# Seven more heads per layer: probabilities times values as one float32 product in place of two split products

## The chip, the cores and the metric

The kernel runs on one core of a Trainium2 chip. The metric is the device time of one execution in microseconds, the median of several runs. Times of single instructions come from one profiled execution of the same kernel.

## The reference, cut to what matters

The program is two transformer blocks on a sequence of 512 tokens, width 1024. The first block has two layers, and each layer is a feed-forward part, a mixer with four groups of attention heads (a: neighbourhood windows, b: low-rank latent, c: difference of two softmaxes, d: grouped queries; four heads of width 64 in each), an output projection, and a second feed-forward part. The second block has one layer with other mixers. What the change touches is the last line of each attention of the first block:

```python
p = jax.nn.softmax(logits, axis=-1).astype(v.dtype)
return jnp.einsum('bhqk,bkhd->bqhd', p, v)
```

All arithmetic is float32. For group a the probabilities of a query are zero outside a window, so there fewer keys count; for group c the weight is the difference of two softmaxes.

## The kernel before

TensorE multiplies the type `float32r` (the code's F32R) at a higher rate than float32, with fewer bits. Most products are therefore split: a number is a high part `hi` (a float32r copy, made on ScalarE) and a low part `lo` (the number minus `hi`, made on VectorE or GpSimd), and the product is three float32r matmuls (`Builder.mm3`, lines 99 to 101; line 442 in the projections; line 323 in the feed-forward parts).

The mixer of a first-block layer is `mix_layer`. The string `PLAN` (line 975) gives the order in which projections and heads are written, and `schedule` interleaves the stages of the heads, up to five at a time. The heads come in the order c0, c1, c2, c3, b0, b1, d0, b2, b3, d1, d2, a0, d3, a1, a2, a3. The framework's scheduler then sets each engine's order from its own estimates, so an edit in one head can move other instructions; each engine runs its own list in order. Between heads the list of TensorE holds projections (line 442), whose weights ScalarE copies (line 88) and GpSimd subtracts (line 89, `wlo`).

A head has three stages. The first builds the transposed queries and keys (line 518 transposes the tiles `dup`; `st` tiles at lines 525 to 539 and 855 to 862). The second computes four blocks of scores (line 549) and their softmax (lines 559 to 563: a maximum `nm` on VectorE, an exponential `p` on ScalarE). The third is `attend` (line 630): for each of the four key blocks it transposes the probabilities into a PSUM bank of the ring `t` of three (line 642), copies them to SBUF as `pth` on ScalarE, and multiplies them by the values. There are two ways to do that. Which one a head takes is told by the list `NATIVE` (line 408):

```python
native = key in NATIVE
vv = None if native else self.split_v(v, c0, h % 2)
# split: split_p, lines 509 and 510, then pv, lines 575 to 579
nc.scalar.activation(out=h[:, a:z], in_=ps[:, a:z], func=AF.Copy)
nc.vector.tensor_tensor(out=l[:, a:z], in0=ps[:, a:z], in1=h[:, a:z].bitcast(F32), op=ALU.subtract)
for e in range(2):
    nc.tensor.matmul(out=ps[:, a:z], lhsT=vv[:, j], rhs=pts[j][e][:, a:z], ...)
nc.scalar.activation(out=y[r], in_=ps[o], func=AF.Copy)
nc.vector.tensor_tensor(out=y[r], in0=ps[r], in1=y[r], op=ALU.add)
# native: line 649, then pv_native, lines 589 and 590
nc.scalar.activation(out=t[:, a:z], in_=ps[:, a:z], func=AF.Copy)
nc.tensor.matmul(out=ps[r, a:z], lhsT=v[:, j, c0:c0 + 64], rhs=pts[j][:, a:z], ...)
nc.scalar.activation(out=y[r], in_=ps[r], func=AF.Copy)
```

The split way puts the high and low parts of a head's 64 value columns side by side in one tile `vv` of 128 columns (line 501 on ScalarE, line 502 on GpSimd), splits the probabilities into `pth` and `ptl`, runs two float32r matmuls for each key block (line 575), and adds the two halves of the result on VectorE (line 579). The native way uses the float32 values and probabilities as they are, with one float32 matmul for each key block (line 589). The profile records such a float32 matmul as two matmuls, each with a weight load.

Before the change nine of the sixteen heads are native: a0, a1, a3, b1, b3, c1, c3, d1, d3. The other seven are split, in both layers. The forgetting attention of the second block is split too (it calls `attend` without a key).

Of the kernel before, what the change touches and what calls it, by code (L numbers as in the profile page):

```python
# [404 lines left out]
NCOPY = ()  # L405
PVA = ()
QKA = ('a3',)
NATIVE = 'a0,a1,a3,b1,b3,c1,c3,d1,d3'.split(',')

NA_WIN = [(0, 2), (0, 3), (1, 4), (2, 4)]  # L410
NA_OFF = [0, 256, 256, 640]
# [2 lines left out]
class Mixer1:  # L414
# [215 lines left out]
    def attend(self, ys, h, probs, v, c0, win=None, key=None):  # L630

        b, nc = self.b, self.nc
        win = win or [(0, 4)] * 4
        native = key in NATIVE
        vv = None if native else self.split_v(v, c0, h % 2)
# [1387 lines left out]
```

## Time and profile before

| | before |
|---|---|
| median of 3 runs | 2501.27 us (2501.06 to 2502.19) |
| profiled execution: time, span of its instructions | 2497.98 us, 2496.2 us |
| granted TensorE clock, mean | 0.992 |
| PE busy, PEld busy | 2387.0 us (96%), 2074.3 us (83%) |
| DVE, ACT, POOL busy | 1817.4 us (73%), 1270.8 us (51%), 710.3 us (28%) |
| mixer of layer 0, of layer 1 | about 395 to 700 us, about 1432 to 1738 us of the span |

PE is TensorE's matmuls, PEld its weight loads, DVE is VectorE, ACT ScalarE, POOL GpSimd. The end of a matmul is modelled in the profile and matmuls overlap, so what a matmul takes of TensorE's time is read from the start of one to the start of the next. In a row of the timeline, "x6" means that six equal records in a row are merged. In brackets at the end stands the idle time of that engine before the instruction, and what ended it.

### The profile page before, as it was taken

Reading aid. Unit: us, or ns where it says so; the run is one execution under the profiler, and the core shown is the slowest. Engines: PE = TensorE matmul, PEld = TensorE weight load, DVE = VectorE, ACT = ScalarE, POOL = GpSimd, SP = SyncE. Lnnn points to the kernel's source line nnn. Section 1 sums busy time; section 2 is a strip of 40 time slices with the busy share of each in tenths; the row PEclk is TensorE's granted clock in tenths of the full one; section 3 lists DMA queues with packets and bytes.
Section 4 is the critical chain, followed back from the end, with each engine's and each line's share of the span. In section 5 each row is a group of like instructions: output and inputs, shape, how many; then the busy total and the mean of one; then the engine's idle time right before and its main releaser. Section 6 shows DMA issues by size and latency. Waiting matters only on the chain. (4 is left out here: it accounts for less than half of the span.)

```text
span 2496.2 us, 39030 instructions
## 1 busy us (share of the span) xinstructions
PE 2387.0 (96%) x14712; PEld 2074.3 (83%) x14712; DVE 1817.4 (73%) x3247; ACT 1270.8 (51%) x2414; POOL 710.3 (28%) x559
## 2 busy tenths in 40 slices
PE   8999999899999999999999999999999999889998
PEld 6899988776778999888999888767889997678778
DVE  7877776976487777787777689745877777855654
ACT  5444456677443444544444566764444445434474
POOL 2221115652212121302111447323011104453232
PEclk9999999999999999999999999999999999999999
DMA  5333333210323333323332432012333324131111
GB/s 166 107 102 102 95 117 102 89 51 16 98 82 107 105 102 89 94 92 107 105 103 68 134 100 90 20 54 85 102 98 105 103 61 155 59 81 43 41 42 64
DMA packets 113884, 220.55 MB, mean 88 GB/s; under 512 B 22192, under 2 KB 33520, under 8 KB 113696
## 3 DMA queue, kind: packets, MB, share of 16 engines
q1 hardware_dynamic: 110288, 217.74, 28.7%
q8 instruction: 115, 1.88, 0.3%
q10 hardware_dynamic: 3408, 0.33, 0.1%
q14 instruction: 73, 0.60, 0.1%
HBM read 209.14 MB, written 8.78 MB: 87 GB/s over the span
## 5 line engine op out<-in xcount | busy, mean ns | idle before, releaser
L88 ACT ACTIVATE whi<-raw 128x1024 fp32r<-128x1024 f32 (+4 forms) x351 | 271.6, 775 | 488.6 <-PE t L323 205.3
L298 POOL TENSOR_TENSOR xl<-xh,xh 128x512 f32<-128x512 f32 x120 | 175.9, 1469 | 718.0 <-DVE wlo L306 368.3
L323 PE MATMUL t<-fh,wlo 128*128 128x256 f32 x1024 | 288.0, 281 | 2.4 <-DVE wlo L306 2.4
L323 PE MATMUL t<-fh,whi 128*128 128x256 f32 x1024 | 287.6, 281 | 0.0
L323 PE MATMUL t<-fl,whi 128*128 128x256 f32 x1024 | 287.6, 281 | 0.0
L99 PE MATMUL acc<-gh,whi 128*128 128x512 f32 x704 | 274.7, 391 | 7.7 <-DVE x L380 5.2
L100 PE MATMUL acc<-gl,whi 128*128 128x512 f32 x704 | 274.5, 390 | 0.0
L101 PE MATMUL acc<-gh,wlo 128*128 128x512 f32 x704 | 274.3, 390 | 0.2 <-DVE wlo L89 0.2
L89 DVE TENSOR_TENSOR wlo<-raw,whi 128x512 fp32r<-128x512 f32 (+3 forms) x277 | 229.8, 830 | 52.7 <-ACT whi L88 51.2
L89 POOL TENSOR_TENSOR wlo<-raw,whi 128x1024 fp32r<-128x1024 f32 (+2 forms) x74 | 167.8, 2270 | 203.5 <-ACT whi L88 190.6
L323 PE MATMUL s<-fh,whi 128*128 128x256 f32 x768 | 216.3, 282 | 8.0 <-DVE wu L326 8.0
L323 PE MATMUL s<-fh,wlo 128*128 128x256 f32 x768 | 215.8, 281 | 0.0
L323 PE MATMUL s<-fl,whi 128*128 128x256 f32 x768 | 215.7, 281 | 0.0
L323 PEld LDWEIGHTS t<-fh,wlo 128*128 128x128 f32 x1024 | 196.4, 192 | 3.1 <-DVE wlo L306 3.0
L305 ACT ACTIVATE whi<-xh 128x512 fp32r<-128x512 f32 x180 | 113.9, 633 | 165.5 <-issue 85.7
L323 PEld LDWEIGHTS t<-fl,whi 128*128 128x128 f32 x1024 | 192.3, 188 | 5.0
L323 PEld LDWEIGHTS t<-fh,whi 128*128 128x128 f32 x1024 | 192.2, 188 | 5.0
L380 DVE SCALAR_TENSOR_TENSOR x<-acc,x 128x512 f32<-128x512 f32 x184 | 126.5, 687 | 64.4 <-PE acc L101 64.0
L306 DVE TENSOR_TENSOR wlo<-xh,whi 128x512 fp32r<-128x512 f32 x180 | 147.5, 819 | 27.9 <-ACT whi L305 27.8
L442 PE MATMUL acc<-whi,xh 128*128 128x256 f32 (+1 forms) x576 | 165.0, 290 | 2.2 <-DVE gate L1140 1.8
L442 PE MATMUL acc<-wlo,xh 128*128 128x256 f32 (+1 forms) x576 | 166.4, 290 | 0.1
L442 PE MATMUL acc<-whi,xl 128*128 128x256 f32 (+1 forms) x576 | 165.9, 290 | 0.0
(724 smaller groups left out, 6535.8 us busy)
## 6 DMA issues: line engine op xcount, KB each, us to landing
xh<-in_ffn_gu_dram SPq DMA_DIRECT2D x240, 256.0 KB
raw<-in_ffn_d_dram SPq DMA_DIRECT2D x128, 256.0 KB
raw<-in_ffn_gu_dram SPq DMA_DIRECT2D x48, 512.0 KB
raw<-in_w2f_dram SPq DMA_DIRECT2D x25, 512.0 KB
raw<-in_ffn_d_dram SPq DMA_DIRECT2D x64, 192.0 KB
xs<-x SPq DMA_DIRECT2D x24, 256.0 KB
raw<-in_a_dram SPq DMA_DIRECT2D x12, 512.0 KB
x<-xs SPq DMA_DIRECT2D x24, 256.0 KB
```

The source lines that it names most:

```text
L88: nc.scalar.activation(out=hi, in_=raw, func=AF.Copy)
L89: (lo_eng or self.lo_eng).tensor_tensor(out=lo, in0=raw, in1=hi.bitcast(F32), op=ALU.subtract)
L99: mm(out=out, lhsT=lh, rhs=rh, start=start, stop=False)
L100: mm(out=out, lhsT=lh, rhs=rl, start=False, stop=False)
L101: mm(out=out, lhsT=ll, rhs=rh, start=False, stop=stop)
L298: eng.tensor_tensor(out=o, in0=x, in1=y, op=op)
L305: nc.scalar.activation(out=hi[:, c], in_=src, func=AF.Copy)
L306: nc.vector.tensor_tensor(out=lo[:, c], in0=src, in1=hi[:, c].bitcast(F32), op=ALU.subtract)
L323: nc.tensor.matmul(out=out, lhsT=x[:, k], rhs=y[:, j], start=start and k == 0 and n == 0, stop=stop and k == 3 and n == 2, skip_group_chec ...
L380: nc.vector.scalar_tensor_tensor(out=x, in0=ps, scalar=0.5, in1=x, op0=ALU.mult, op1=ALU.add)
L442: mm = lambda l, r, st=False, sp=False: nc.tensor.matmul(out=ps[i], lhsT=l, rhs=r, start=st, stop=sp, skip_group_check=True)
```

## The change

The list names all sixteen heads. So the heads a2, b0, b2, c0, c2, d0 and d2 of both layers go the native way.

```diff
-NATIVE = 'a0,a1,a3,b1,b3,c1,c3,d1,d3'.split(',')
+NATIVE = [m + h for m in 'abcd' for h in '0123']
```

What this does to the lists of the engines is shown at three places of layer 0.

VectorE, head c0, while the softmaxes of head c1 and the projections of group b stand beside it. Before:

```order
L753 TENSOR_TENSOR t_948_4755<-t_948_4755,rt_4789 128x8x32
L510 TENSOR_TENSOR ptl_5035<-t_5029,pth_5034 128x512
L466 TENSOR_SCALAR hms_4820<-hms_4820 128x4
L890 TENSOR_SCALAR c_1015_4983<-c_1015_4983,sums_4270,c_nl_4261 128x1
L510 TENSOR_TENSOR ptl_5044<-t_5038,pth_5043 128x512
L465 TENSOR_REDUCE hms_4851<-sq_971_4849 128x4
L892 SCALAR_TENSOR_TENSOR p_4979<-p_4986,c_1015_4983,p_4979 128x512
```

and now:

```order
L753 TENSOR_TENSOR t_948_4755<-t_948_4755,rt_4789 128x8x32
L466 TENSOR_SCALAR hms_4820<-hms_4820 128x4
L890 TENSOR_SCALAR c_1015_4983<-c_1015_4983,sums_4270,c_nl_4261 128x1
L465 TENSOR_REDUCE hms_4851<-sq_971_4849 128x4
L892 SCALAR_TENSOR_TENSOR p_4979<-p_4986,c_1015_4983,p_4979 128x512
```

The subtractions that make `ptl` are gone from between the other work; over the program VectorE's list loses 70 instructions (56 of line 510, 14 of line 579), GpSimd's the 14 of line 502, and ScalarE's the 14 of line 501.

TensorE, the products of head c0 among the projections. Before:

```order
L442 MATMUL acc_5373<-wlo_5431,xh_758_3949 128x256
L575 MATMUL t_5065<-pth_5034,vv_5026 128x512
L575 MATMUL t_5065<-ptl_5035,vv_5026 128x512
L575 MATMUL t_5065<-pth_5043,vv_5026 128x512
L575 MATMUL t_5065<-ptl_5044,vv_5026 128x512
L442 MATMUL acc_5373<-whi_5430,xl_759_3950 128x256
```

and now:

```order
L442 MATMUL acc_5340<-wlo_5399,xh_751_3924 128x256
L589 MATMUL t_5054<-pth_5031,cv_4321 64x512
L589 MATMUL t_5054<-pth_5038,cv_4321 64x512
L442 MATMUL acc_5340<-whi_5398,xl_752_3925 128x256
L442 MATMUL acc_5340<-whi_5398,xh_758_3949 128x256
```

Four float32r matmuls have become two float32 ones of half as many output rows, and they stand some matmuls earlier among the projections.

TensorE, head d0, where the `dup` tiles belong to a later head. Before:

```order
L575 MATMUL t_6439<-pth_6426,vv_6400 128x512
L575 MATMUL t_6439<-ptl_6427,vv_6400 128x512
L518 MATMUL t_6458<-ident_150,dup_6450 128x128
L518 MATMUL t_6458<-ident_150,dup_6452 128x128
L518 MATMUL t_6458<-ident_150,dup_6454 128x128
L518 MATMUL t_6458<-ident_150,dup_6456 128x128
L575 MATMUL t_6439<-pth_6435,vv_6400 128x512
```

and now:

```order
L549 MATMUL s_6418<-st_6316,st_6308 128x512
L589 MATMUL t_6380<-pth_6371,dv_5333 64x512
L518 MATMUL t_6394<-ident_150,dup_6386 128x128
L518 MATMUL t_6394<-ident_150,dup_6388 128x128
L518 MATMUL t_6394<-ident_150,dup_6390 128x128
L518 MATMUL t_6394<-ident_150,dup_6392 128x128
L589 MATMUL t_6380<-pth_6378,dv_5333 64x512
```

The products no longer stand in one run: scores of another head lie between the second and the third, so the four float32 products form three groups.

## Rows read from the trace of the kernel before

**Rows 1.** Stretches: length, busy us of PE, PEld, DVE, ACT, POOL; clock, DMA.
```profile
440.00:530.00 90.00, 81.73 (x570) 72.75 (x570) 88.23 (x222) 61.56 (x142) 62.07 (x54) 0.96 0.27 83
530.00:690.00 160.00, 153.26 (x819) 112.20 (x817) 93.82 (x210) 96.92 (x209) 43.69 (x40) 1.00 0.18 55
1477.00:1567.00 90.00, 79.90 (x565) 71.26 (x564) 89.06 (x214) 59.74 (x138) 61.51 (x52) 0.98 0.24 80
...
450.00:460.00 10.00, 6.94 (x33) 6.21 (x34) 9.88 (x22) 5.92 (x13) 4.39 (x3) 0.66 0.33 107
```

**Rows 2.** Waits of PE, 440 to 690: total us, times, longest.
```profile
PE s L549 <- DVE nm L562: 3.9, 2, 2.5
PE t L642 <- DVE st L526: 2.8, 4, 0.9
PE t L518 <- DVE dup L490: 2.3, 1, 2.3
PE t L642 <- DVE ptl L510: 2.0, 2, 1.7
...
PE t L518 <- DVE y L579: 0.3, 1, 0.3
```

**Rows 3.** The same view of layer 1, 1477 to 1727.
```profile
PE t L642 <- DVE ptl L510: 2.9, 3, 2.0
```

**Rows 4.** Timeline of the split product: start, us, engine, instruction (d0, then a2).
```profile
569.50 0.40 PE L575 MATMUL t<-ptl,vv 128*128 128x512 f32 x1
569.73 0.39 PE L575 MATMUL t<-pth,vv 128*128 128x512 f32 x1
...
649.18 0.34 PE L575 MATMUL t<-ptl,vv 128*128 128x384 f32 x1
649.36 0.29 PE L575 MATMUL t<-pth,vv 128*128 128x256 f32 x1
649.48 0.28 PE L575 MATMUL t<-ptl,vv 128*128 128x256 f32 x1
```

**Rows 5.** Timeline of the native product, with the row behind it (d1, then a1).
```profile
594.51 1.93 PE L589 MATMUL t<-pth,dv 128*64 128x512 f32 x4
596.37 0.50 PE L549 MATMUL s<-st,st 128*128 128x256 f32 x2
596.80 1.07 PE L589 MATMUL t<-pth,dv 128*64 128x512 f32 x2
597.81 1.16 PE L136 MATMUL t<-sel,ysq 128*128 128x128 f32 x8
...
640.37 0.86 PE L589 MATMUL t<-pth,av 128*64 128x384 f32 x2
641.16 0.50 PE L100 MATMUL acc<-xl,whi 128*128 128x512 f32 x1
...
645.07 0.65 PE L589 MATMUL t<-pth,av 128*64 128x256 f32 x2
645.65 1.16 PE L136 MATMUL t<-sel,ysq 128*128 128x128 f32 x8
```

**Rows 6.** Groups by line of VectorE, 440 to 690: busy us, mean ns, idle before.
```profile
L510 DVE TENSOR_TENSOR ptl<-t,pth 128x512 fp32r<-128x512 f32 x24 | 16.3, 684 | 1.3 <-ACT pth L509 1.1
L579 DVE TENSOR_TENSOR y<-t,y 64x512 f32<-64x512 f32 x7 | 4.7, 678 | 0.9 <-ACT y L578 0.9
```

**Rows 7.** The line that makes `vv` on GpSimd: duration min/median/max.
```profile
L502 POOL TENSOR_TENSOR vv<-cv,vv x4: 741/744/752, 405.9 to 1443.7; 128x256 fp32r<-128x256 f32 x4
```

**Rows 8.** Timelines of DVE, POOL and PE where PE stops in layer 0.
```profile
447.24 2.60 DVE L752 TENSOR_TENSOR t<-t,b_cos 128x256 f32<-128x256 f32 x1
...
446.73 2.83 POOL L89 TENSOR_TENSOR wlo<-raw,whi 128x1024 fp32r<-128x1024 f32 x1
...
451.35 0.50 PE L549 MATMUL s<-st,st 96*128 96x512 f32 x1 [2.45 <-DVE nm L562]
...
455.31 1.12 PE L642 MATMUL t<-ident,p 128*128 128x128 f32 x4 [1.71 <-DVE ptl L510]
```

## The prediction

> **What bounds the kernel now.** I read the stretches of the two mixers first, since the change touches nothing else. A mixer has two phases. In the first, 440 to 530 us in layer 0 and 1477 to 1567 in layer 1, VectorE is busy 88.2 and 89.1 of 90 us and TensorE 81.7 and 79.9 [rows 1]: both are full, and TensorE has 8.3 and 10.1 us of idle. In the second, 530 to 690, TensorE is busy 153.3 of 160 us and VectorE 93.8 [rows 1]: TensorE sets the pace, with 6.7 us of idle. So per layer TensorE has some 15.0 us of idle (8.3 + 6.7), and the rest is its own work. Second, the waits of TensorE say who ends that idle time. In layer 0 the softmax maxima take 3.9 us, a query stack of line 526 2.8, a `dup` tile 2.3, `ptl` 2.0 and the addition of line 579 0.3 [rows 2]; in layer 1 `ptl` takes 2.9 [rows 3]. Only `ptl` and line 579 are removed by the change. Third, the timeline tells what the long stops are made of. A VectorE multiply took 2.60 us from 447.24 while a GpSimd subtraction of 2.83 us ran from 446.73, and TensorE then stood 2.45 us for a maximum from VectorE, and soon after 1.71 us for `ptl` [rows 8]. In the ten microseconds of these two stops the granted clock fell to 0.66 [rows 1], a mixture of 1.2 and 2.4 GHz, and was back at 1.00 for the phase behind it.
>
> **The price on TensorE.** Matmul time is counted from start to start.
>
> - Split, 512 columns: 569.50 to 569.73 is 0.23 us [rows 4]; a head has 4 key blocks of 2 matmuls, 8 x 0.23 = 1.84 us.
> - Native, 512 columns: a run of two products (four records) takes 594.51 to 596.37, 1.86 us, and one product by itself 596.80 to 597.81, 1.01 us [rows 5]. Head d1 consists of such a run and two single ones: 1.86 + 1.01 + 1.01 = 3.88 us. In runs alone a head would take 3.72, in single products 4.04. The list of d0 after the change shows one run and two single products, so I take 3.88. A head costs 3.88 - 1.84 = 2.04 us more (1.88 to 2.20).
> - Head a2 has two blocks of 384 columns and two of 256. Split: 649.18 to 649.36 and 649.36 to 649.48, 0.18 and 0.12 us [rows 4], 4 x 0.18 + 4 x 0.12 = 1.20. Native: 640.37 to 641.16 and 645.07 to 645.65, 0.79 and 0.58 us a product [rows 5], 2 x 0.79 + 2 x 0.58 = 2.74. More by 1.54.
> - Per layer six heads of the first kind and one a2: 6 x 2.04 + 1.54 = 13.8 us; both layers **27.6 us** (25.7 to 29.5 with the bounds).
>
> This work lies on TensorE's own list in stretches that it fills to 91% and 96%, so it counts in full, and what follows says how much is given back.
>
> **What is given back.**
>
> - Waits that ended with an instruction that goes: `ptl` 2.0 and 2.9, line 579 0.3, together 5.2 us. Next late in these places is ScalarE's copy `pth`, which came just before `ptl`; it had to be there anyway. I credit **5**; half of it, if the copy holds the bank nearly as long.
> - The clock. It fell after two stops in layer 0, and the second ended with `ptl` [rows 8]. Without it the fall may not come. A share of 0.66 over ten microseconds in which TensorE was busy 6.9 [rows 1] costs 0.34 x 6.9 = 2.3 us; I credit **2** (0 to 2.3).
> - VectorE. In a layer it loses 24 subtractions and seven additions, 16.3 + 4.7 = 21.0 us of the 88.2 + 93.8 that it is busy [rows 6, 1], some 12%, and the four smaller subtractions of a2. Other VectorE results that TensorE waits for come sooner by part of that. Those waits are 3.9 + 2.8 + 2.3 = 9.0 us in layer 0 [rows 2], and I take layer 1 for the same, 18 in all. The bounds are 0 and 18. The two largest follow a VectorE instruction held beside a GpSimd subtraction of weights [rows 8], and those subtractions all stay; the waits for line 526 lie in a phase where VectorE has room. So I take a third, **6**.
> - GpSimd loses 14 subtractions of 0.74 us [rows 7] and ScalarE 14 copies. Both run long before they are needed (a head's `vv` is made while its scores are), nothing on TensorE is seen to wait for them, and I give them nothing. No DMA is added or removed; a few weight loads stand elsewhere in the queue, with no wait of TensorE on them in these stretches.
>
> Sum: 27.6 - 5 - 2 - 6 = **+14.6 us**. The profiled execution took 2498.0 us, so it would take 2512.6; the median stands 3.3 us above it, at 2501.3, and so the forecast is 2515.9, in round numbers **2515 us**.
>
> On the held instruction there is a rule to weigh. The row alone says that one of VectorE's multiplies took 2.60 us while GpSimd was at work [rows 8], and I priced the removal of GpSimd's `vv` at nothing. The Trainium skill, page "SBUF — State Buffer", section "Who interferes with whom", says that VectorE with two inputs in SBUF and a GpSimd instruction that reads SBUF shut each other out for the length of an instruction. The trace agrees in this row: the long multiply ends just after the GpSimd instruction. By that rule the 14 `vv` subtractions could each hold VectorE for up to their own length, 14 x 0.74 = 10.4 us, and the sum would be +9 if TensorE waited for a half of that. It also says that an instruction with at most one SBUF input is not held, and the `ptl` subtraction has one (its other is PSUM), so by it the removed subtractions never were among the held ones. No row shows a `vv` subtraction holding anything that TensorE waited for, so the sum goes without it.
>
> **The rivals.**
>
> *VectorE sets the pace, and the kernel gets faster.* Place: both first phases. For it: 88.2 of 90 us busy there, and the longest stops of TensorE end with VectorE [rows 1, 2]. Then less VectorE work shortens the phase, TensorE's added work fills idle time, and in the second phase the waits go as well. Its most is all the idle time of the mixer, 15.0 us a layer, and the 2 us of clock in a layer, 17.0 against 13.8 added: 3.2 less a layer, 6.4 in both, **2495 us**. It decides where idle falls below 15.0 - 13.8 + 2 = 3.2 us a layer or so. Against it: in the second phase TensorE is 96% busy, five of the seven heads lie there (b0, b2, d0, d2, a2), and their 4 x 2.04 + 1.54 = 9.7 us find only 6.7 us of idle, partly ended by ScalarE or by TensorE's own order.
>
> *They cancel.* Four fifths or more of the idle goes, 12 us a layer, with one fall of the clock: 27.6 - 24 - 2 = +1.6, **2503 us**. For it: the removed instructions stand between the softmax work that TensorE waits for. Against it as above.
>
> *Nothing comes back.* The scheduler's new order puts the float32 products where they break other runs, and a new late result takes the place of `ptl`: 29.5 - 2.5 = +27, **2528 us**. For it: the lists moved in all of the mixer. Against it: two falls of VectorE's load can hardly give nothing.
>
> That the change leaves heads as they were is ruled out by the lists: 56 of the 72 instructions of line 510 are gone, and the 16 that stay are the second block's.
>
> **How the numbers follow.** A measurement of this kernel can tell about 0.2%, 5 us, from no change: "same" is 2496.3 to 2506.3. Forecast, a net price of 5 to 22 us: 0.60. Cancel: 0.18. VectorE sets the pace: 0.12. Nothing comes back: 0.10. Faster 0.12, same 0.18, slower 0.70. The range reaches down through most of the case that cancels, to 2501 (the low price with all the 18, 5.2 and 2.3 given back: 25.7 - 25.5 = +0.2), and up to 2526, just short of the case with nothing back; it leaves out the faster case and about 0.08 above.
>
> **What would show it.** In the profile after: line 575 with 16 matmuls of each kind, the second block's; line 589 with 56 products more, 112 records; busy time of VectorE down by about 42 us over the program. Right, if TensorE's idle in the mixers falls by 4 to 9 us a layer, with no wait for `ptl` left, and the phase from 530 to 690 is longer by 4 to 8 us. Wrong, if the phase from 440 to 530 gets shorter by more than 5 us and the idle of both phases nearly vanishes (faster), or if the waits for line 562 and line 490 grow and the granted clock falls at more places than before (slower than the range). The price term is wrong if a native head takes less than 3.7 or more than 4.1 us from its first product to the end of its last, without what lies between.

## The result

The change made the kernel slower: 2520.38 us (median of 5 runs, 2517.96 to 2523.72) against 2501.27, a ratio of 1.0072 with a 95% interval of 1.0062 to 1.0083, or +18.0 us of 2501.3. The forecast was 2515 us, with a range of 2501 to 2526. The kernel before was timed beside it, five times by now (2496.94 to 2503.39 us); its profile is still the one shown ahead. The profiled execution of the change took 2522.31 us, its span is 2520.5.

The page of the profile after, part 1 (busy time, share of the span, instructions of each engine):

```profile
PE 2421.3 (96%) x14712; PEld 2069.7 (82%) x14712; DVE 1775.5 (70%) x3177; ACT 1265.3 (50%) x2400; POOL 698.0 (28%) x545
```

VectorE is busy 41.9 us less (1817.4 before), in 70 instructions fewer; TensorE is busy 34.3 us more, with as many records, since two float32r matmuls became two records of one float32 product.

The stretches of layer 0 after (columns as in [rows 1]: length, busy us of PE, PEld, DVE, ACT, POOL, granted clock, DMA):

```profile
440.00:530.00 90.00, 84.00 (x535) 65.67 (x534) 79.54 (x219) 58.44 (x135) 56.79 (x51) 0.96 0.26 83
530.00:690.00 160.00, 155.41 (x809) 106.52 (x808) 75.22 (x168) 90.84 (x200) 38.45 (x34) 1.00 0.16 49
450.00:460.00 10.00, 9.23 (x36) 5.23 (x36) 9.89 (x26) 6.65 (x16) 5.57 (x4) 0.83 0.40 130
480.00:490.00 10.00, 9.48 (x38) 4.87 (x38) 9.97 (x35) 8.06 (x23) 7.13 (x8) 0.83 0.33 103
```

Beside [rows 1] the reader sees VectorE fall from 88.2 to 79.5 and from 93.8 to 75.2 us, and TensorE's idle time from 8.3 to 6.0 and from 6.7 to 4.6. In the same 250 us the idle time is 4.4 us less, and TensorE has not finished: the mixer goes on to 701.8 us, where it ended at 691.2 before. The clock of these two profiles is not better: where one stretch of ten microseconds stood at 0.66 there are now two at 0.83, the same 3.4 us of clock.

To see a whole mixer I take from its first matmul of line 442 to the last addition of line 1014 in each layer and let the profile add both up. Before (364.2 to 691.2 and 1401.7 to 1729.7 us):

```profile
sum 655.00, PE 620.62 PEld 505.76 DVE 472.94 ACT 419.04 POOL 293.20; mean PE 310.31 PEld 252.88 DVE 236.47 ACT 209.52 POOL 146.60
```

After (363.7 to 701.8 and 1414.4 to 1751.1):

```profile
sum 674.80, PE 650.05 PEld 496.15 DVE 430.90 ACT 413.71 POOL 280.30; mean PE 325.03 PEld 248.08 DVE 215.45 ACT 206.86 POOL 140.15
```

The mixers are 19.8 us longer. TensorE is busy 29.4 us more in them and idle 24.8 us in place of 34.4, 9.6 less: 29.4 - 9.6 = 19.8. The rest of the span is 1841.2 us before and 1845.7 after, where nothing was changed; runs of one kernel scatter by as much, and the mean granted clocks of the two profiled executions, 0.992 and 0.990, differ by about 5 us of 2500 (an estimate: 0.002 x 2500, if TensorE is busy all the time).

Work also moved between the phases. The last product of the c heads starts 173.2 and 173.8 us behind the begin of its mixer before, and 162.0 and 161.3 us after; behind it the mixer still has 30 and 33 projection matmuls (line 442) before, and 122 and 121 after. So stretches at fixed times do not hold the same work in the two kernels. Split at that product, TensorE's idle time falls in both phases: from 8.9 and 10.1 to 6.4 and 6.6 us in the first, from 7.8 and 7.7 to 6.2 and 5.6 us in the second.

The waits of TensorE after, 440 to 700 us (total us, times, longest), to be held against [rows 2]:

```profile
PE s L549 <- DVE nm L562: 2.7, 2, 2.5
PE t L589 <- ACT pth L649: 1.8, 1, 1.8
PE t L642 <- DVE st L526: 1.5, 1, 1.5
PE t L642 <- DVE st L862: 1.5, 1, 1.5
...
PE t L642 <- ACT pth L649: 0.6, 2, 0.3
```

The waits for `ptl` and for the addition of line 579 are gone, those for `dup` too, and those for lines 562 and 526 are shorter. In their place stand waits for ScalarE's copy `pth` (1.8 and 0.6 us) and for the stack of line 862 (1.5). The long one for `pth` ends at 480.52 us, at a product of a c head, and the second stretch of low clock above, 480 to 490 us, comes right behind it:

```profile
480.52 1.07 PE L589 MATMUL t<-pth,cv 128*64 128x512 f32 x2 [1.75 <-ACT pth L649]
```

The product of head d0 after, with the rows behind it:

```profile
572.82 1.93 PE L589 MATMUL t<-pth,dv 128*64 128x512 f32 x4
574.68 1.67 PE L549 MATMUL s<-st,st 96*128 96x512 f32 x6
576.28 1.07 PE L589 MATMUL t<-pth,dv 128*64 128x512 f32 x2
577.29 0.66 PE L518 MATMUL t<-ident,dup 128*128 128x128 f32 x4
577.87 1.07 PE L589 MATMUL t<-pth,dv 128*64 128x512 f32 x2
578.88 0.66 PE L642 MATMUL t<-ident,p 128*128 128x128 f32 x4
```

From start to start it is 1.86 + 1.01 + 1.01 = 3.88 us, what the forecast took from [rows 5].

### The profile page after: what moved, and what is told of

The parts are those of the page before. It is cut to its first block, busy times and chain, and to the rows that moved or that the text cites. A ratio compares the mean times of both kernels' runs of the same rounds, so it can differ in the third digit from the quotient of the medians.

```text
span 2520.5 us, 38923 instructions
## 1 busy us (share of the span) xinstructions
PE 2421.3 (96%) x14712; PEld 2069.7 (82%) x14712; DVE 1775.5 (70%) x3177; ACT 1265.3 (50%) x2400; POOL 698.0 (28%) x545
## 5 line engine op out<-in xcount | busy, mean ns | idle before, releaser
L305 ACT ACTIVATE whi<-xl 128x512 fp32r<-128x512 f32 x240 | 143.2, 620 | 44.5 <-PE t L323 40.8
```

What stands on the lines that cost most here:

```text
L305: nc.scalar.activation(out=hi[:, c], in_=src, func=AF.Copy)
```

## The experiments

Three theories were held against each other. A: TensorE sets the pace, the length of the native product is the cost, and VectorE's relief gives some of it back. B: VectorE sets the pace of each mixer's first phase. C: what counts is the new order of the lists. Each kernel ran beside the kernel before on the same chip, and the ratios are to that.

### The subtraction of `ptl` alone

```diff
-                pts.append(self.split_p(ps, a, z))
+                if key is None:
+                    pts.append(self.split_p(ps, a, z))
+                else:
+                    hi = self.t("pth", dt=F32R)
+                    nc.scalar.activation(out=hi[:, a:z], in_=ps[:, a:z], func=AF.Copy)
+                    pts.append((hi, hi))
```

> The kernel before, with the subtraction that makes ptl left out in the seven split heads of the first block; the second matmul of each key block reads the high part pth again, so the low part of the probabilities is missing from the product. TensorE's work stays as it is, VectorE loses 56 subtractions (about 36 us of its busy time). Theory A (TensorE sets the pace, the native product's length is the cost, VectorE's relief gives back little): 5 to 9 us faster, 2492 to 2496. Rival B (VectorE sets the pace of the first phase of each mixer): 12 us faster or more, 2489 or less. Rival C (neither counts, the scheduler's new order does): within 3 us of before, or slower.

Measured: 2499.69 us, ratio 0.9989 (0.998 to 0.9997), 2.8 us faster (0.8 to 5.0). That is less than A expected and none of B's 12 us; by the number alone it is what C expected. The two mixers:

```profile
sum 652.30, PE 621.30 PEld 503.13 DVE 443.47 ACT 420.02 POOL 292.44; mean PE 310.65 PEld 251.57 DVE 221.73 ACT 210.01 POOL 146.22
```

VectorE is busy 29.5 us less in them and TensorE idle 31.0 us in place of 34.4. The waits for `ptl` are gone, but in layer 0 other waits stand in their place (1.5 us for a stack of line 865, 0.8 for `pth`). So 56 subtractions of VectorE are worth little by themselves, at least in the order that the lists have here.

### The price alone

```diff
-            for e in range(2):
+            for e in range(times):
...
-    nc.tensor.matmul(out=ps[:, a:z], lhsT=vv[:, j], rhs=pts[j][e][:, a:z], ...)
+    nc.tensor.matmul(out=ps[:, a:z], lhsT=vv[:, j], rhs=pts[j][e % 2][:, a:z], ...)
```

with `times` 4 in the first block and 2 elsewhere.

> The kernel before, with each key block's two split matmuls run twice into the same bank in the seven split heads (the sum is doubled, which the norm behind it takes out again). That adds TensorE work of 12 heads x 8 x 0.23 + 2 x 1.20 = 24.5 us and takes nothing from VectorE. Theory A: nearly all of it shows, +19 to +25, 2520 to 2526. Rival B: the four heads c0 and c2 hide theirs in TensorE's idle time of the first phase, +15 to +18, 2516 to 2519. Rival C: no sum holds, the new order decides.

(The norm covers four heads, so the doubling of some of them is not quite taken out.) Measured: 2528.32 us, ratio 1.0108 (1.0093 to 1.0123), +27.0 us for 24.5 us of added matmuls, 2 us above A's range. The two mixers:

```profile
sum 679.60, PE 644.76 PEld 524.84 DVE 478.53 ACT 419.30 POOL 290.58; mean PE 322.38 PEld 262.42 DVE 239.27 ACT 209.65 POOL 145.29
```

They are 24.6 us longer, TensorE is busy 24.1 us more, and its idle time is 34.8 us in place of 34.4. Work added to TensorE is paid in full; over the two mixers none of it filled idle time, so the c heads' share did not either. This is A, and it is against B.

### The heads in two groups

```diff
-NATIVE = 'a0,a1,a3,b1,b3,c1,c3,d1,d3'.split(',')
+NATIVE = 'a0,a1,a3,b1,b3,c1,c3,d1,d3,c0,c2'.split(',')
```

> Of the change only c0 and c2 go native (both layers), the two in the phase where VectorE is full. Added TensorE work 4 x 2.04 = 8.2 us. Theory A: about half comes back, +3 to +6, 2504 to 2507. Rival B: VectorE's 13 us less shorten the phase, 3 us or more faster, 2498 or less. Rival C: as much as the whole change, +10 or more, since the order of the phase moves as in the whole change.

```diff
-NATIVE = 'a0,a1,a3,b1,b3,c1,c3,d1,d3'.split(',')
+NATIVE = 'a0,a1,a3,b1,b3,c1,c3,d1,d3,b0,b2,d0,d2,a2'.split(',')
```

> Of the change only b0, b2, d0, d2 and a2 go native (both layers), the five in the phase where TensorE is full. Added TensorE work 8 x 2.04 + 2 x 1.54 = 19.4 us. Theory A: 4 to 8 us come back, +11 to +15, 2512 to 2517; with the run of the two c heads it adds up to the whole change. Rival B: these heads carry more than the whole change, +19 or more, 2520 or more, and the c heads give some back. Rival C: under +6, the loss sits where the order of the first phase moves.

Measured: the c heads 2501.85 us, ratio 1.0001 (0.9991 to 1.001); the five others 2517.62 us, ratio 1.0062 (1.005 to 1.0074), +15.5 us, at the upper end of what A expected. Their sum, +15.8, is the whole change within the intervals. The two mixers with c0 and c2 native:

```profile
sum 656.20, PE 629.17 PEld 503.54 DVE 453.93 ACT 417.36 POOL 288.94; mean PE 314.59 PEld 251.77 DVE 226.96 ACT 208.68 POOL 144.47
```

TensorE is busy 8.6 us more (8.2 were forecast) and idle 27.0 us in place of 34.4. In these heads, where VectorE is full, the price came back, and more of it than A expected; in the five others about a fifth did (15.5 of the 19.4 us of price remain). B's gain is not there either.

### Relief without price

The native flow with float32r probabilities and values, the product run twice. VectorE, GpSimd and ScalarE have the load of the change, or nearly (ScalarE keeps its copy of the values), and TensorE the split way's matmuls. Once for c0 and c2, once for all seven heads (`TWICE`).

```diff
+        if key in TWICE:
+            vr = self.t("vv", (P, 4, 64), F32R)
+            nc.scalar.activation(out=vr, in_=v[:, :, c0:c0 + 64], func=AF.Copy)
...
-                t = self.t("pth")
+                t = self.t("pth", dt=F32R if key in TWICE else F32)
...
-            nc.tensor.matmul(out=ps[r, a:z], lhsT=v[:, j, c0:c0 + 64], ...)
+            for e in range(times):
+                nc.tensor.matmul(out=ps[r, a:z], lhsT=v[:, j, c0:c0 + 64], ...)
```

> What c0 and c2 give back when nothing is paid: the native flow in these two heads (no ptl, no vv on GpSimd, no addition), but with float32r probabilities and values and the 64-row product run twice, so TensorE's work stays at the split way's 8 x 0.23 us a head; the low parts are missing and the sum is doubled. If the relief of the other engines is worth the 7 to 8 us that came back: 2494 to 2496. If TensorE's added work only filled idle time that nothing else can shorten: within 3 us of before, 2499 to 2505.

> The same for all seven heads of the change: all that the change takes from VectorE, GpSimd and ScalarE, and none of the price on TensorE. By the sum on record 13 us faster, 2489; by the result of the change (27.6 us of price, 19 of loss) 8 to 9, 2493; by the two runs without ptl 3 or less, 2499 or more. If 2493 comes out, price and relief simply add up to the change; if 2499, the price on TensorE is partly filled into idle time instead.

Measured: c0 and c2 2495.05 us, ratio 0.9973 (0.9964 to 0.9983), -6.8 us; all seven 2488.93 us, ratio 0.995 (0.9938 to 0.9962), -12.5 us. The two mixers of the latter:

```profile
sum 644.30, PE 617.68 PEld 498.96 DVE 427.37 ACT 416.31 POOL 283.91; mean PE 308.84 PEld 249.48 DVE 213.69 ACT 208.16 POOL 141.95
```

This is the give-back by itself: 12.5 us (9.5 to 15.5), where the forecast had credited 13. Against it the change is +18.0, so the native products cost about 30.5 us where the forecast had 27.6 (the two intervals together leave some 26 to 35); in the two profiles the mixers differ by 674.8 - 644.3 = 30.5 too, and TensorE's busy time by 650.1 - 617.7 = 32.4. About half of the relief comes from two of the seven heads, those in the phase where VectorE is full.

Part of this relief is the clock. The mean granted clock of the executions on record is 0.9891 for the kernel before (17 of them) and 0.9916 with all seven relieved (5); 0.0025 x 2500 is 6 us, an estimate that holds if TensorE is busy all the time. In layer 0 the profile has no low clock in the first phase, though the stop for the maximum is there as before, and as long (lines are one further down in this kernel):

```profile
450.84 0.50 PE L550 MATMUL s<-st,st 96*128 96x512 f32 x1 [2.50 <-DVE nm L563]
```

```profile
440.00:530.00 90.00, 82.28 (x570) 69.92 (x569) 85.78 (x233) 63.92 (x147) 63.06 (x55) 1.00 0.27 88
```

### The subtraction put back

Native heads in which VectorE still makes a `ptl` that nobody reads: in all seven, and in c0 and c2 alone (there with only c0 and c2 added to the list).

```diff
+                if key in ('a2', 'b0', 'b2', 'c0', 'c2', 'd0', 'd2'):
+                    l = self.t("ptl", dt=F32R)
+                    nc.vector.tensor_tensor(out=l[:, a:z], in0=ps[:, a:z], in1=t[:, a:z], op=ALU.subtract)
                 pts.append(t)
```

> The change with VectorE's load of before put back: in the seven heads that went native, VectorE still subtracts the copy from the bank for every key block (here float32 from float32, so zeros, into a tile that nobody reads). TensorE's work is that of the change. The two halves of what VectorE gives back are told apart: if its load is what counts, 4 to 9 us over the change, 2524 to 2529; if it was the wait of the product for ptl, which stays gone here, no more than 2 us over the change, 2518 to 2522.

> The run of the two c heads with VectorE's 16 subtractions put back (zeros, into a tile that nobody reads). That run came out even although TensorE had 8.2 us more work. If the subtractions' place on VectorE is what paid for it: about 6 to 8 us slower than before, 2508 to 2510. If it was the rest (product no longer waiting for ptl, the addition of line 579, GpSimd's and ScalarE's vv): even with before, 2500 to 2504.

Measured: all seven 2520.67 us, ratio 1.0081 (1.0067 to 1.0094), within the interval of the change; c0 and c2 2508.26 us, ratio 1.0033 (1.0023 to 1.0044), against 1.0001 without the subtraction. By these numbers the load on VectorE is what paid in the c heads, while in the seven it hardly shows; the two do not fit one price for a subtraction. Nor is the loss in the c heads mainly idle time: in the mixers of the two profiles TensorE is idle 27.0 us without the subtraction and 28.5 with it, and busy 629.2 and 633.4 us.

And the subtraction left out in c0 and c2, the rest split:

```diff
-                pts.append(self.split_p(ps, a, z))
+                if key not in ('c0', 'c2'):
+                    pts.append(self.split_p(ps, a, z))
...
+                    pts.append((hi, hi))
```

> The kernel before, with the subtraction that makes ptl left out in c0 and c2 alone (the second matmul reads pth again, so the low part is missing there). TensorE's work stays, VectorE loses 16 subtractions (11 us) where it is full. The run of the two c heads cost 8.2 us of TensorE and came out even, so 7 to 8 us came back there. Theory A (the subtractions in VectorE's full phase are what came back): 4 to 7 us faster, 2495 to 2498. Rival D (it came from the rest that goes: GpSimd's vv, the addition of line 579, or a lucky order): within 2 us of before, 2500 to 2504.

Measured: 2503.89 us, ratio 1.0005 (0.9996 to 1.0014). No gain, where the c heads' whole relief is worth 6.8 us. So which of the removed instructions pays is not settled by these four runs: taking `ptl` out of c0 and c2 gives nothing, putting it back costs 8 us, and the order of all lists moves in both.

### The other way

```diff
-NATIVE = 'a0,a1,a3,b1,b3,c1,c3,d1,d3'.split(',')
+NATIVE = 'c0,c1,c2,c3'.split(',')
```

> The other way: only the four c heads are native, all of a, b and d are split. Against before c0 and c2 go native (even, by the run of the two c heads), and b1, b3, d1, d3, a0, a1, a3 go split: TensorE loses 8 x 2.04 + 6 x 1.54 = 25.6 us and VectorE gains 14 heads of subtractions in the phase where it has room. Theory A, with a quarter lost again as in the run of the five heads: about 19 us faster, 2480 to 2486. Rival E (split heads make TensorE wait for ptl and for the ring of banks in that phase, so that they are worth their price): 2497 or more.

```diff
-NATIVE = 'a0,a1,a3,b1,b3,c1,c3,d1,d3'.split(',')
+NATIVE = ()
```

> No head is native: as the run with only the c heads native, with c0 to c3 split too. TensorE loses another 16.3 us, VectorE gains 8 heads of subtractions and additions where it is full. Theory A with VectorE as the pace of the first phase: even with the run of the c heads or up to 6 us slower, 2480 to 2492. If the first phase goes by TensorE alone: 10 us or more faster than that run.

```diff
-NATIVE = 'a0,a1,a3,b1,b3,c1,c3,d1,d3'.split(',')
+NATIVE = 'c1,c3'.split(',')
```

> Only c1 and c3 native, all else split: between the run with no native head (2498.9) and the one with four c heads (2487.0). If each c head is worth the same: 2493. If VectorE is the pace of the first phase until two heads are relieved: 2487 to 2490, as the two further heads came out even in the kernel before too.

Measured: four c heads 2487.0 us, ratio 0.9937 (0.9924 to 0.995), just outside what was expected; none 2498.85, ratio 0.999 (0.9981 to 0.9999); c1 and c3 2489.01, ratio 0.9956 (0.9944 to 0.9968), as expected if two relieved heads are enough. The two mixers with no native head:

```profile
sum 652.80, PE 595.97 PEld 519.60 DVE 524.03 ACT 422.63 POOL 305.75; mean PE 297.98 PEld 259.80 DVE 262.01 ACT 211.32 POOL 152.88
```

with c1 and c3:

```profile
sum 643.70, PE 602.40 PEld 516.27 DVE 511.05 ACT 422.94 POOL 302.69; mean PE 301.20 PEld 258.13 DVE 255.52 ACT 211.47 POOL 151.35
```

with the four c heads:

```profile
sum 639.20, PE 604.92 PEld 507.88 DVE 487.42 ACT 421.31 POOL 300.82; mean PE 302.46 PEld 253.94 DVE 243.71 ACT 210.65 POOL 150.41
```

The series shows both sides of the bargain, busy and idle time of TensorE in the two mixers:

| native heads per layer | busy us | idle us | length us |
|---|---|---|---|
| none | 596.0 | 56.8 | 652.8 |
| c1, c3 | 602.4 | 41.3 | 643.7 |
| c0 to c3 | 604.9 | 34.3 | 639.2 |
| nine (before) | 620.6 | 34.4 | 655.0 |
| sixteen (the change) | 650.1 | 24.8 | 674.8 |

Eight more native heads should add 8 x 2.04 = 16.3 us of work, but only 8.9 show. Part of the difference is the clock: in layer 0, 450 to 530 us, it is 0.96 with no native head and 1.00 with the four c heads:

```profile
450.00:530.00 80.00, 68.69 (x491) 64.22 (x492) 79.01 (x199) 52.63 (x124) 54.13 (x46) 0.96 0.26 85
```

```profile
450.00:530.00 80.00, 74.37 (x475) 57.88 (x474) 70.48 (x211) 54.68 (x125) 54.52 (x48) 1.00 0.27 87
```

That is 80 x 0.04 = 3.2 us of clock in one layer, and VectorE falls from 79.0 to 70.5 of 80 us there. The mean granted clock of the executions on record agrees: 0.986 with no native head, 0.990 with the four c heads (0.989 before). So the c heads take away 22.5 us of idle time for 8.9 us of busy time, the higher clock counted in. The other heads are another matter: from the four c heads to all sixteen, busy time grows by 45.1 us and idle time falls by 9.5. (The nine of before are not a step between: of the c heads they hold c1 and c3 alone.) Four c heads, or two, beat both kernels: 0.6% and 0.4% under the kernel before, with intervals that overlap each other. My guess for the kernel with no native head was too low (2480 to 2492): I had held the c heads for a break-even everywhere, and where all else is split they are worth 12 us, of which the clock can be up to 10 (0.004 x 2500, an estimate as above).

## Why the prediction held, step by step

*Which way, and why.* Right. TensorE's own work sets the length of the mixers, and added matmuls show one for one (24.6 us of mixer for 24.1 us of busy time in the run of the price alone).

*The price of a head.* 3.88 us for a native head was forecast, and d0 took 3.88 in the profile after. The sum of 27.6 us looks some 3 us too small: two profiles of nearly equal load on the other engines differ by 30.5 us, though the intervals of the times do not exclude 27.6. Two things had been left out of it. The first is the entry into a native product, seen among the projections of the profile after:

```profile
456.30 0.28 PE L442 MATMUL acc<-wlo,xh 128*128 128x256 f32 x1
456.42 0.28 PE L442 MATMUL acc<-whi,xl 128*128 128x256 f32 x1
456.62 1.07 PE L589 MATMUL t<-pth,cv 128*64 128x512 f32 x2
```

A projection matmul that takes 0.12 us to the next one takes 0.20 when a native product follows; 0.08 us for three groups in each of 12 heads is 2.9 us. The same 0.09 us or so is seen in front of native products elsewhere, behind transposes (0.20 in place of 0.11) and scores (0.33 in place of 0.24); the split products show no such delay (0.12 behind a projection matmul). The second is that head c0 now stands in a stretch of low clock:

```profile
450.77 0.56 PE L549 MATMUL s<-st,st 96*128 96x512 f32 x1 [2.51 <-DVE nm L562]
...
452.33 2.98 PE L589 MATMUL t<-pth,cv 128*64 128x512 f32 x4
455.24 0.39 PE L442 MATMUL acc<-whi,xl 128*128 128x256 f32 x1
```

Its first two products took 2.91 us in place of 1.86, and the whole head 2.91 + 1.01 + 1.01 = 4.93 us, more than the 4.1 that the forecast had named as the sign of a wrong price; the clock is what it lacked there. The two additions lead to some 32 us, near the 32.4 us by which TensorE is busier than in the run of relief without price. That run had no low clock in this stretch; against the kernel before, whose head c0 stood in low clock too, the second addition does not all count.

*The clock.* Wrong in its reading. The forecast said that the clock fell after two stops and that without the second, the one for `ptl`, the fall might not come. In the trace before, that second stop ended at 455.31 us after 1.71 us [rows 8], and the clock was down before it began, while TensorE still worked (the stop begins at 453.60 us; the clock of this microsecond, 0.50, is the lower of its two levels):

```profile
453.00:454.00 1.00, 0.60 (x4) 0.30 (x2) 1.00 (x1) 0.23 (x1) 1.00 (x1) 0.50 0.00 0
```

So the fall did not need `ptl`. In the profile after it comes again behind the stop for the maximum, but shorter (0.83 over the same ten microseconds in place of 0.66), and a second one stands behind the wait for `pth` that ends at 480.52 us. What was gained at the one place was lost at the other: in these two profiles nothing came back of the 2 us in layer 0. The profile before is a good one, though: its clock is 0.992, where the executions of that kernel in the three series of experiments have 0.989 on the mean, and the five of the change have 0.991. So a gain that the two profiles do not show is possible. In layer 0 of the relief without price the same stop for the maximum is followed by no fall; that stop alone does not bring the clock down either, and what does stays open.

The stop for the maximum that the forecast found in [rows 8] is there again, and so is what led to it, in the VectorE and GpSimd timelines of the profile after:

```profile
446.67 2.58 DVE L752 TENSOR_TENSOR t<-t,b_cos 128x256 f32<-128x256 f32 x1
```

```profile
446.16 2.81 POOL L89 TENSOR_TENSOR wlo<-raw,whi 128x1024 fp32r<-128x1024 f32 x1
```

The multiply is held by the weight subtraction as in [rows 8] and ends 0.3 us after it. This is the rule of the Trainium skill, page "SBUF — State Buffer", section "Who interferes with whom"; the trace agrees a second time. A `vv` subtraction does hold VectorE now and then. In layer 1 of the trace before, a multiply of two tiles in SBUF took 0.78 us beside one, where the next of its kind took 0.18 (GpSimd's row, then VectorE's):

```profile
1560.35 0.74 POOL L502 TENSOR_TENSOR vv<-dv,vv 128x256 fp32r<-128x256 f32 x1
...
1560.36 0.78 DVE L930 TENSOR_TENSOR rt<-t,d_sin 128x32 f32<-128x32 f32 x1
1561.06 0.18 DVE L929 TENSOR_TENSOR rt<-t,d_sin 128x32 f32<-128x32 f32 x1
1561.16 0.18 DVE L930 TENSOR_TENSOR rt<-t,d_sin 128x32 f32<-128x32 f32 x1
```

Only three of the 14 show such a hold of 0.2 us or more in that trace, and the 10.4 us that the rule allowed for did not appear on top of the sum.

*Waits that go, and VectorE's relief.* 5 + 6 us were credited, with the clock 13. All of the relief without the price measured 12.5. The total was right, and in its parts that is partly luck. The run without the subtraction of `ptl` takes away the waits for `ptl` (4.9 of the 5 us) and 16.3 of VectorE's 21.0 us a layer; by the forecast's own terms it should have gained 4.9 + 6 x 16.3 / 21.0 = 9.6 us, and it gained 2.8. In the change the waits for `ptl` and line 579 vanished, but 2.4 us of waits for `pth` and 1.5 for line 862 came in layer 0. Up to 6 of the 12.5 us go with the clock, for which the forecast had 2. What else gives the 12.5 (GpSimd's `vv`, the addition of line 579, the narrower weights, the order of the lists) no run tells apart. The relief is uneven: 6.8 us from c0 and c2, 5.7 from the five others.

*The rivals.* That VectorE sets the pace and the change is faster did not come true: idle time fell from 17.2 to 12.4 us a layer in the mixer, not to a few. The phase was named rightly; only there the heads come out even. That nothing comes back is refuted by the run without price. That they cancel holds for the c heads alone.

*The signs named ahead.* Line 510 has 16 instructions left, VectorE is 41.9 us less busy (42 forecast), idle time fell by 4.8 us a layer over whole mixers and by 4.4 in 440 to 690 us (4 to 9 forecast), no wait for `ptl` is left. Two signs can't be read as they were meant: some 90 projection matmuls a layer moved behind the c heads, so the first phase, up to their last product, is 11 to 13 us shorter and the second 21 or 22 longer, where 4 to 8 had been named. And the low clock at two places in place of one in layer 0 was named as a sign of more than the range, but the waits for lines 562 and 490 did not grow.

What stays open is which of the removed instructions pays, since an edit of one moves the order of all lists, what part of the relief is the clock's, and whether the order by itself is worth some microseconds (theory C); no run was made that changes the order and nothing else.

## What to carry to other kernels

Where a product can be made long on TensorE or split on the others, decide for each place in the program, by who is full there: in the phase where VectorE was full, four heads as one float32 product took away 22.5 us of TensorE's idle time for 8.9 us more of its busy time; in the phase where TensorE was 96% busy the heads cost about four fifths of what their matmuls are longer (15.5 of 19.4 us). A run that adds only the price and one that gives only the relief tell more than the change itself. Here they nearly add up to it: +27.0 us for 24.5 us of added matmuls, 3.1 us more because the native products are priced at 27.6, and -12.5 make +17.6, where +18.0 was measured. And the removal of a wait or of one instruction need not be worth its own length: without `ptl` 4.9 us of waits went, others came, and 2.8 us were gained.

## What the runs showed of the hardware

The float32 product of 64 output rows holds TensorE 0.93 us for 512 columns in a run of two, against 0.46 for two float32r matmuls, and lets the matmul in front of it take 0.08 us longer. Its weight loads are shorter (0.136 us each, against 0.188 for the 128 columns of `vv`), and PEld's busy time in the mixers fell from 505.8 to 496.2 us while the mixers grew by 19.8: here neither it nor the share of busy TensorE (96% before and after) tells which kernel is the faster.
